# A windowed-attention and SwiGLU layer on one core: the softmax sink as a 129th key, a group's norm in four pieces, and another PSUM buffer for the transposed probabilities

## The chip, the cores and the metric

One core of a Trainium2 chip runs the whole layer. The metric is the time on the device, in microseconds (us), from the start to the end of one execution; the value of a kernel is the median of several runs. The engines are named as in the profile: PE is the matrix engine (PEld its weight loads), DVE the vector engine, ACT the scalar engine, POOL the GpSimd engine, SP the engine that only issues transfers. All data is float32; products on PE are made in split form, high part and low part.

## What is computed

The input x has 512 rows (tokens) of 2048. With one layer, only attention and the feed-forward part run:

```python
h = rms_norm(x, mixer_norm)
x = x + sliding_window_attention(h, ...)      # 32 query heads of 64, 4 key/value heads, window 128
x = x + swiglu(rms_norm(x, ffn_norm), ...)    # 2048 -> 5632 -> 2048
```

Inside attention, for each block of 128 queries, its own 128 keys and the 128 before them:

```python
scores = einsum('bnqhgd,bnkhd->bnhgqk', qb, kw) * scale      # masked to the window
m = maximum(max(scores), sink)                               # one sink number per head
p = exp(scores - m)
probs = p / (sum(p) + exp(sink - m))
out = einsum('bnhgqk,bnkhd->bnqhgd', probs, vw)
```

Queries and keys are normed per head (mean square over the 64 numbers) and rotated before the scores.

## The kernel before

The program is one list of events. `ev(t, fn)` puts a piece of code at time t, counted in weight tiles (256 rows by 512 columns of a weight matrix), and `run_events` calls the pieces in order of t. PE executes in that order. The order on DVE and ACT is not that of the calls: after the first four tiles a scheduler orders both engines when the program is built, by its own estimate of what is ready; `soon()` gives a piece a high priority in it. POOL and SP keep queues of their own. Each engine works its queue strictly in order.

The first 40 weight tiles make keys and values (tiles 0 to 7) and then queries, 8 tiles for each of the four key/value groups; tiles from 40 on are the output projection. One weight tile is 24 products of 128x512 (`tok_mm`, L144 in the profile), and ACT and DVE split each tile into `whi` and `wlo` ahead of it.

The attention of a group g is laid between the products of the next tiles, in class `Group`. E is the event time at which the group's queries are complete. `evac` copies them out of PSUM; `stat` squares them on ACT, sums the squares on DVE (`qss`) and makes the factor `f8` with `head_factor`, 13 short DVE operations each needing the one before; `q_prep` rotates a block's queries (POOL makes `rt`, DVE multiplies and adds into `qraw`) and splits them into `qs`; `k_exp` and `k_tr` do the same for the keys (`kx`, `kT`). A group has eight units, called u0 to u7 here: four blocks b, two halves hf of four heads. The units of the next group are marked with a prime, so u0' follows u7. The stretch in which u4 to u7 of one group, the norm of the next and its u0' and u1' come together is called a turn; there are three, in order turn 1, 2 and 3. A unit's chain is:

- `q_tr`: PE transposes four heads' queries into a PSUM tile, ACT copies them to `qT`;
- `soft`: PE makes the scores `sc`; ACT copies the last 128 keys' columns to `p`; DVE puts the earlier keys' columns over them where the mask says so (the predicated copy); DVE finds the maximum `mx`; ACT takes the exponentials with their sum `sm`; DVE divides;
- `p_tr`: PE transposes `p` into the PSUM tile `pT`; ACT copies the high part `ph`, DVE makes the low part `pl`; POOL selects `uh` and `ul` from them for the earlier block's keys;
- `pv`: PE multiplies with the values into the PSUM tile `po`, in four products (`ph`, `pl`, `uh`, `ul`); ACT (`oh`) and DVE (`attT`) bring it out.

PSUM has eight banks. Four hold the running products (`accA`), two the scores (`psc`, one buffer of two banks), and two are the buffers of `pst`, tag t1, in turn for `ptr` of queries, `ptr` of keys, `pT` and `po`. An engine that writes a new tile into a buffer waits until all readers of the old tile are done. The events of a unit stand at u - 0.78 (`q_tr`), u (`soft`), u + 1.43 (`p_tr`) and u + 1.99 (`pv`), with u 0.98 apart from unit to unit, so `p_tr` of one unit falls between the scores of the next two.

Of the kernel before, what the change touches and what calls it, by code (L numbers as in the profile page):

```python
# [19 lines left out]
P = 128  # L20
# [4 lines left out]
HD = 64  # L25
# [21 lines left out]
def hybrid_layer(ctx, tc, x, positions, inv_freq, mixer_norm, ffn_norm, w_qkv, q_norm, k_norm, sinks,  # L47
# [136 lines left out]
    nsink = cp.tile([P, 32], F32, name="nsink")  # L184
# [13 lines left out]
    warm = ap_.tile([P, 512], F32R, tag="qT", name="warm", bufs=3)  # L198
# [86 lines left out]
    tabs = {}  # L285

    def tables():
        dve.tensor_scalar(nsink, sink_b, -1.0, None, ALU.mult)
# [137 lines left out]
    class Group:  # L426
# [8 lines left out]
                copy_r(qr, qb[self.g + 1][t])  # L435
                self.qraw.append(qr)

        def stat(self):
            qss = ap_.tile([P, 32], F32, tag="qss", name="qss", bufs=2)
            for t in range(NT):  # L440
                sq = ap_.tile([P, 512], F32, tag="sq", name="sq")
                act.activation(sq, self.qraw[t], AF.Square)
                dve.tensor_reduce(qss[:, 8 * t:8 * t + 8], sq.rearrange("p (h d) -> p h d", d=HD), AX.X, ALU.add)
            fa = ap_.tile([P, 32], F32, tag="fa", name="fa")
            fb = ap_.tile([P, 32], F32, tag="fb", name="fb")
            self.f8 = ap_.tile([P, 32], F32, tag="f8", name="f8", bufs=2)
            head_factor(self.f8, qss, fa, fb, rs8, 8)

        def k_exp(self):
            g = self.g  # L450
            kx = ap_.tile([P, 2, NT, 2, HD], F32R, tag="qs", name="kx", bufs=2)
            s4 = kc[:, :, g * HD:(g + 1) * HD].unsqueeze(2).to_broadcast([P, NT, 2, HD])
            copy_r(kx[:, 0], s4)
            sub(kx[:, 1], s4, kx[:, 0].bitcast(F32))
            self.kx = kx
# [19 lines left out]
        def q_tr(self, b, hf):  # L475
            ptr = pst.tile([P, 512], F32R, tag="t1", name="ptr")
            for h in range(4):
                pe.transpose(ptr[:, h * P:(h + 1) * P],
                             self.qs[b][:, hf * 4 + h, :, :].rearrange("p c d -> p (c d)"), identr)
            qT = ap_.tile([P, 512], F32R, tag="qT", name="qT", bufs=3)  # L480
            with soon():
                copy_r(qT, ptr.bitcast(F32))
            self.qT[b, hf] = qT

        def soft(self, b, hf):

            h0 = self.g * GRP + hf * 4
            sc = psc.tile([P, 4, 256], F32, tag="sc", name="sc")
            lo_ = 0 if b else P
            qT = self.qT.pop((b, hf))  # L490
            for h in range(4):
                q_ = qT[:, h * P:(h + 1) * P]
                ks = slice((b - 1) * P + lo_, (b + 1) * P)
                mm(sc[:, h, lo_:256], q_, self.kT[0][:, ks], True, False)
                mm(sc[:, h, lo_:256], q_, self.kT[1][:, ks], False, True)
            p_ = ap_.tile([P, 4, P], F32, tag="p", name="p", bufs=3)
            mb = mask.unsqueeze(1).to_broadcast([P, 4, P])
            with soon():
                copy_r(p_, sc[:, :, P:256])
                if b:  # L500
                    dve.copy_predicated(p_, mb, sc[:, :, 0:P])
                else:
                    dve.copy_predicated(p_, mb, negc.unsqueeze(2).to_broadcast([P, 4, P]))
            mx = ap_.tile([P, 4], F32, tag="mx", name="mx", bufs=3)
            sm = ap_.tile([P, 4], F32, tag="sm", name="sm", bufs=3)
            es = ap_.tile([P, 4], F32, tag="es", name="es", bufs=3)
# [11 lines left out]
            dve.tensor_tensor(p_, p_, sm.unsqueeze(2).to_broadcast([P, 4, P]), ALU.mult)  # L518
            self.p[b, hf] = p_

        def p_tr(self, b, hf):
            p_ = self.p.pop((b, hf))
            pT = pst.tile([P, 512], F32, tag="t1", name="pT")
            for h in range(4):
                pe.transpose(pT[:, h * P:(h + 1) * P], p_[:, h, :], ident)  # L525
# [12 lines left out]
            self.pt[b, hf] = (ph, pl, pu)  # L538
# [19 lines left out]
                dve.tensor_tensor(attT[up, b, kt0:kt0 + 2, :], o4[up, :, 1, :], oh[up], ALU.add)  # L558

    LAG, PACE, TQ, QP = 2.6, 0.98, 0.78, 1.39  # L560
    TT, TP = 1.43, 1.99
    KX, KA, KB = 3.03, 1.98, 0.28
    for g in range(NKV):
        G = Group(g)
        E = 8 * (g + 2)
        ev(E - 0.0005, G.evac)
        ev(E + 0.01, G.stat)
        ev(E - KX, G.k_exp)
        ev(E - KA, lambda G=G: G.k_tr(0))
        ev(E - KB, lambda G=G: G.k_tr(1))  # L570
# [619 lines left out]
```

## Time and profile before

| | |
|---|---|
| median of 3 runs | 1877.29 us (1876.54 to 1877.72) |
| the profiled execution | 1877.08 us, span 1875.4 us |
| mean granted clock of PE | 0.997 |
| busy in the span | PE 1851.9 us, DVE 1500.3, ACT 878.2, POOL 146.8 |
| chain that ended last, by engine | PE 88%, DVE 7%, ACT 3% |

Busy time is the sum of an engine's instructions; matmuls are pipelined, so a busy PE can still lose a little at each stop. The chain that ended last is followed back from the last instruction, at each step to what released it. PE is busy in nearly all of the span; the attention units lie between 120 and 400 us.

### The profile page before, as it was taken

What the parts mean: (1) busy time and instruction counts of PE and PEld (TensorE: products, weight loads), DVE (VectorE), ACT (ScalarE), POOL (GpSimd) and SP (SyncE); (2) the same over time, 40 slices, a digit from 0 to 9 for tenths busy, and PEclk for the clock granted to TensorE, in tenths of its full rate; (3) what the DMA queues carried; (4) which work ended last, traced back from release to release, by engine and by line L of the source; (5) the groups of instructions that cost most, each with busy time, mean ns of one, the idle gap of its engine ahead of it and who ended that gap; (6) DMA issues with size and microseconds to landing.
All of it is one profiled execution on the core that took longest, in us unless ns stands there. A gap on an engine that the chain in (4) does not pass through costs nothing.

```text
span 1875.4 us, 32539 instructions
## 1 busy us (share of the span) xinstructions
PE 1851.9 (99%) x13118; PEld 1735.8 (93%) x13118; DVE 1500.3 (80%) x2422; ACT 878.2 (47%) x1347; POOL 146.8 (8%) x183
## 2 busy tenths in 40 slices
PE   8999999999999999999999999999999999999999
PEld 6887877788889999999999999999998999899899
DVE  4568898864686888888888888888889888988987
ACT  5458788754453333334333333433435434534532
POOL 0012122110000000000000000000000011012011
PEclk8999999999999999999999999999999999999999
DMA  6322211134413333333333333333345556646664
GB/s 205 90 79 59 67 56 59 66 128 170 168 57 96 124 119 119 124 115 122 113 113 123 125 114 120 118 113 116 125 131 186 163 133 151 198 127 137 175 183 135
DMA packets 162967, 230.81 MB, mean 123 GB/s; under 512 B 10141, under 2 KB 109537, under 8 KB 162305
## 3 DMA queue, kind: packets, MB, share of 16 engines
q1 hardware_dynamic: 146400, 194.81, 32.1%
q0 software_dynamic: 15552, 32.61, 7.6%
q8 instruction: 102, 1.67, 0.4%
q10 hardware_dynamic: 864, 1.33, 0.2%
q14 instruction: 49, 0.39, 0.1%
HBM read 200.39 MB, written 31.46 MB: 124 GB/s over the span
## 4 chain that ended last, share of the span: by engine, by line
PE 88%; DVE 7%; ACT 3%; issue 1%; DMA 1%; POOL 0%; ACTq 0%; DVEq 0%
PE acc L144 85%; PE sc L144 1%; DVE wlo L70 1%; PE po L144 1%; ACT p L513 1%; DVE hlo L70 0%; DVE dwl L70 0%; PE pT L525 0%; DVE sums L70 0%; PE pt L691 0%; DVE pl L70 0%; PE pt L250 0%; DVE mx L507 0%; DMA raw<-actd 0%; DVE sl L70 0%
## 5 line engine op out<-in xcount | busy, mean ns | idle before, releaser
L65 ACT ACTIVATE Whi<-W 128x1792 fp32r<-128x1792 f32 x168 | 286.5, 1705 | 518.3 <-PE acc L144 263.0
L70 DVE TENSOR_TENSOR Wlo<-W,Whi 128x1792 fp32r<-128x1792 f32 x168 | 340.4, 2026 | 133.2 <-ACT Whi L65 129.0
L144 PE MATMUL acc<-sh,Wlo 128*128 128x256 f32 x1344 | 380.3, 283 | 0.0
L144 PE MATMUL acc<-sh,Whi 128*128 128x256 f32 x1344 | 380.3, 283 | 0.0
L144 PE MATMUL acc<-sl,Whi 128*128 128x256 f32 x1344 | 380.3, 283 | 0.0
L144 PE MATMUL acc<-hhi,Wlo 128*128 128x256 f32 x1008 | 285.4, 283 | 0.5 <-DVE Wlo L70 0.5
L144 PE MATMUL acc<-hlo,Whi 128*128 128x256 f32 x1008 | 285.3, 283 | 0.0
L144 PE MATMUL acc<-hhi,Whi 128*128 128x256 f32 x1008 | 285.3, 283 | 0.0
L144 PEld LDWEIGHTS acc<-sh,Wlo 128*128 128x128 f32 x1344 | 258.0, 192 | 0.0
L144 PEld LDWEIGHTS acc<-sh,Whi 128*128 128x128 f32 x1344 | 258.0, 192 | 0.0
L144 PEld LDWEIGHTS acc<-sl,Whi 128*128 128x128 f32 x1344 | 258.0, 192 | 0.0
L144 PE MATMUL acc<-whi,hhi 128*128 128x512 f32 x512 | 209.0, 408 | 0.8 <-ACT hhi L67 0.8
L144 PE MATMUL acc<-whi,hlo 128*128 128x512 f32 x512 | 202.3, 395 | 0.0
L144 PE MATMUL acc<-wlo,hhi 128*128 128x512 f32 x512 | 201.5, 394 | 0.0
L144 PEld LDWEIGHTS acc<-hhi,Wlo 128*128 128x128 f32 x1008 | 193.5, 192 | 0.7 <-DVE Wlo L70 0.7
L144 PEld LDWEIGHTS acc<-hhi,Whi 128*128 128x128 f32 x1008 | 193.5, 192 | 0.0
L144 PEld LDWEIGHTS acc<-hlo,Whi 128*128 128x128 f32 x1008 | 193.5, 192 | 0.0
L70 DVE TENSOR_TENSOR W<-W 128x512 f32<-128x512 f32 x336 | 185.9, 553 | 7.6 <-DMA W<-ffn_w_up_in 1.1
L144 PE MATMUL acc<-dwh,sh 128*128 128x256 f32 (+1 forms) x600 | 180.1, 300 | 0.2 <-ACT row L65 0.2
L144 PE MATMUL acc<-dwl,sh 128*128 128x256 f32 (+1 forms) x600 | 180.0, 300 | 0.0
L144 PE MATMUL acc<-dwh,sl 128*128 128x256 f32 (+1 forms) x600 | 180.0, 300 | 0.0
L144 PE MATMUL acc<-dwh,hlo 128*128 128x256 f32 (+1 forms) x500 | 150.1, 300 | 0.0
(288 smaller groups left out, 3572.1 us busy)
## 6 DMA issues: line engine op xcount, KB each, us to landing
W<-ffn_w_up_in SPq DMA_DIRECT2D x176, 256.0 KB, 3.1
dw<-ffn_w_down_in SPq DMA_DIRECT2D x88, 512.0 KB, 3.6
W<-ffn_w_gate_in SPq DMA_DIRECT2D x160, 256.0 KB, 3.0
wraw<-attn_w_qkv_in SPq DMA_DIRECT2D x39, 512.0 KB, 3.6
wraw<-attn_w_o_in SPq DMA_DIRECT2D x32, 512.0 KB, 3.5
actd<-U POOLq DMA_DIRECT2D x22, 512.0 KB, 3.5
raw<-actd SPq DMA_DIRECT2D x22, 512.0 KB, 4.4
x1d<-row POOLq DMA_DIRECT2D x44, 256.0 KB, 5.7
```

The costliest lines, as they stand in the source:

```text
L65: act.activation(dst, src, AF.Copy)
L70: dve.tensor_tensor(dst, a, b, ALU.subtract)
L144: pe.matmul(ps, lhsT, rhs, start=start, stop=stop, skip_group_check=True)
L513: act.activation(p_[:, h, :], p_[:, h, :], AF.Exp, bias=mx[:, h:h + 1], scale=ff[:, h:h + 1], accum_out=sm[:, h:h + 1])
```

## The change

- **Sink.** The tile `p` gets a 129th column per head. POOL fills it with the sink divided by the unit's factor (`sf`), so that the maximum over 129 columns and the exponentials' sum over 129 columns already hold the sink. Three DVE operations on 128x4 numbers per unit (the minimum with `nsink`, `es`, and the addition to `sm`) and one exponential on ACT go; a POOL copy of 128x4 per unit comes. The maximum is multiplied by `nf`, the negated factor.
- **Norm.** `stat` runs once per token tile, at E + 0.01, 0.31, 0.61 and 0.91, and `factor` at E + 1.3 makes `f8`, `nf` and `sf`: three more DVE operations on 128x32 numbers per group.
- **PSUM.** `pT` is no longer a t1 tile; it takes the one scores buffer, so scores, `pT`, scores, `pT` follow each other in it.
- **Keys.** `kx` has a tile of its own in place of a `qs` buffer; `k_exp` moves from E - 3.03 to E - 3.9, the two `k_tr` from E - 1.98 and E - 0.28 to E - 2.83 and E - 1.85.
- `p` and `qT` go from three buffers to two; `pv` from u + 1.99 to u + 2.04.

```diff
-        def stat(self):
-            qss = ap_.tile([P, 32], F32, tag="qss", name="qss", bufs=2)
-            for t in range(NT):
-                sq = ap_.tile([P, 512], F32, tag="sq", name="sq")
-                act.activation(sq, self.qraw[t], AF.Square)
-                dve.tensor_reduce(qss[:, 8 * t:8 * t + 8], sq.rearrange("p (h d) -> p h d", d=HD), AX.X, ALU.add)
+        def stat(self, t):
+            if t == 0:
+                self.qss = ap_.tile([P, 32], F32, tag="qss", name="qss", bufs=2)
+            sq = ap_.tile([P, 512], F32, tag="sq", name="sq")
+            act.activation(sq, self.qraw[t], AF.Square)
+            dve.tensor_reduce(self.qss[:, 8 * t:8 * t + 8], sq.rearrange("p (h d) -> p h d", d=HD), AX.X, ALU.add)
+
+        def factor(self):
...
+            head_factor(self.f8, self.qss, fa, fb, rs8, 8)
+            dve.tensor_scalar(self.nf, self.f8, -1.0, None, ALU.mult)
+            dve.reciprocal(self.sf, self.f8)
+            sv = self.sf.rearrange("p (t h) -> p t h", h=GRP)
+            dve.tensor_tensor(sv, sv, sink_b[:, self.g * GRP:(self.g + 1) * GRP].unsqueeze(1)
+                              .to_broadcast([P, NT, GRP]), ALU.mult)
...
-            kx = ap_.tile([P, 2, NT, 2, HD], F32R, tag="qs", name="kx", bufs=2)
+            kx = ap_.tile([P, 2, NT, 2, HD], F32R, tag="kx", name="kx")
...
-            p_ = ap_.tile([P, 4, P], F32, tag="p", name="p", bufs=3)
+            p_ = ap_.tile([P, 4, P + 4], F32, tag="p", name="p", bufs=2)
+            pk, pa = p_[:, :, 0:P], p_[:, :, 0:P + 1]
+            pool.tensor_copy(p_[:, :, P:P + 1], self.sf[:, f_].unsqueeze(2))
...
-            dve.tensor_reduce(mx, p_, AX.X, ALU.max)
-            ff = self.f8[:, 8 * b + 4 * hf:8 * b + 4 * hf + 4]
-            dve.tensor_tensor(mx, mx, ff, ALU.mult)
-            dve.scalar_tensor_tensor(mx, mx, -1.0, nsink[:, h0:h0 + 4], ALU.mult, ALU.min)
-            dve.tensor_tensor(es, sink_b[:, h0:h0 + 4], mx, ALU.add)
+            dve.tensor_reduce(mx, pa, AX.X, ALU.max)
+            dve.tensor_tensor(mx, mx, self.nf[:, f_], ALU.mult)
             for h in range(4):
-                act.activation(p_[:, h, :], p_[:, h, :], AF.Exp, bias=mx[:, h:h + 1],
+                act.activation(pa[:, h, :], pa[:, h, :], AF.Exp, bias=mx[:, h:h + 1],
                                scale=ff[:, h:h + 1], accum_out=sm[:, h:h + 1])
-            act.activation(es, es, AF.Exp)
-            dve.tensor_tensor(sm, sm, es, ALU.add)
...
-            pT = pst.tile([P, 512], F32, tag="t1", name="pT")
+            pT = psc.tile([P, 4, 256], F32, tag="sc", name="pT")[:, 0:2, :].rearrange("p a b -> p (a b)")
...
-    TT, TP = 1.43, 1.99
-    KX, KA, KB = 3.03, 1.98, 0.28
+    TT, TP = 1.43, 2.04
+    KX, KA, KB = 3.9, 2.83, 1.85
...
-        ev(E + 0.01, G.stat)
+        for t in range(NT):
+            ev(E + 0.01 + 0.3 * t, lambda G=G, t=t: G.stat(t))
+        ev(E + 1.3, G.factor)
```

The scheduler answers to this with another order on DVE. In turn 2, before the low part `pl` of u4 (pl_2524 before), DVE has the first sum of squares and the rotation of the next group's first block:

```order
L507 TENSOR_REDUCE mx_2457<-p_2454 128x4
...
L511 TENSOR_TENSOR es_2459<-sink_b_82,mx_2457 128x4
L443 TENSOR_REDUCE qss_2554<-sq_2555 128x8
L341 TENSOR_TENSOR qraw_2531<-qraw_2531,t1q_465 128x512
L342 TENSOR_TENSOR qraw_2531<-qraw_2531,rt_2593 128x512
L70 TENSOR_TENSOR pl_2524<-pT_2518,ph_2523 128x512
L516 TENSOR_TENSOR sm_2458<-sm_2458,es_2459 128x4
```

With the change the same three operations stand behind it (pl_2476 is now the low part of u4, p_2417 is u5's probabilities, p_2539 u6's):

```order
L516 TENSOR_REDUCE mx_2421<-p_2417 128x4
...
L70 TENSOR_TENSOR pl_2476<-pT_2470,ph_2475 128x512
L521 RECIPROCAL sm_2422<-sm_2422 128x4
L522 TENSOR_TENSOR p_2417<-p_2417,sm_2422 128x4x128
L70 TENSOR_TENSOR wlo_2496<-wraw_2302,whi_2495 128x512 x2
L442 TENSOR_REDUCE qss_2506<-sq_2507 128x8
L339 TENSOR_TENSOR qraw_2483<-qraw_2483,t1q_463 128x512
L511 COPY_PREDICATED p_2539<-mask_86,sc_2530 128x4x128
L442 TENSOR_REDUCE qss_2506<-sq_2516 128x8
L340 TENSOR_TENSOR qraw_2483<-qraw_2483,rt_2522 128x512
```

One sum and two wide operations have moved from ahead of `pl` of u4 to behind it. Further on in turn 2, DVE comes to u0' (p_2768) and to the low part of u7 (pl_2804) with the change like this:

```order
L348 TENSOR_TENSOR f8_2620<-fa_2618,rs8_85 128x32
L513 COPY_PREDICATED p_2768<-mask_86,negc_87 128x4x128
L449 TENSOR_SCALAR nf_2621<-f8_2620 128x32
L450 RECIPROCAL sf_2622<-f8_2620 128x32
L339 TENSOR_TENSOR qraw_2489<-qraw_2489,t1q_463 128x512
L452 TENSOR_TENSOR sf_2622<-sf_2622,sink_b_82 128x32
L70 TENSOR_TENSOR hlo_143<-attT_153,hhi_142 128x4x128
L516 TENSOR_REDUCE mx_2772<-p_2768 128x4
L70 TENSOR_TENSOR wlo_2812<-wraw_2607,whi_2811 128x512
L70 TENSOR_TENSOR pl_2804<-pT_2798,ph_2803 128x512
```

The three new operations of the factor lie on both sides of the predicated copy, and the maximum behind them needs the sink column that POOL copies out of `sf`. Before, `f8` of this group was complete sixteen rows ahead of the same copy.

## Rows read from the trace of the kernel before

**Rows 1.** The page: busy time, share of the span and instructions of each engine.

```profile
PE 1851.9 (99%) x13118; PEld 1735.8 (93%) x13118; DVE 1500.3 (80%) x2422; ACT 878.2 (47%) x1347; POOL 146.8 (8%) x183
```

**Rows 2.** Who PE waited for, whole span: total us, times, longest us.

```profile
PE ptr L460 <- DVE attT L558: 3.1, 3, 1.0
PE pT L525 <- DVE attT L558: 2.9, 4, 0.9
...
PE po L144 <- POOL ul L535: 2.1, 6, 0.4
PE po L144 <- DVE pl L70: 1.9, 2, 1.1
...
PE pT L525 <- ACT qT L65: 1.5, 3, 0.5
```

**Rows 3.** Busy us by stretch: PE, PEld, DVE, ACT, POOL, clock, DMA.

```profile
126.00:134.00 8.00, 8.00 (x47) 6.89 (x46) 3.34 (x9) 5.89 (x15) 0.00 (x0) 1.00 0.23 66
246.00:254.00 8.00, 7.20 (x37) 5.54 (x36) 7.92 (x20) 7.04 (x20) 3.70 (x4) 1.00 0.16 57
...
270.00:278.00 8.00, 6.43 (x35) 4.83 (x34) 7.89 (x20) 6.31 (x21) 1.22 (x2) 1.00 0.20 66
```

**Rows 4.** PE in order of time, turn 2: start, us, tile, [idle before <-releaser].

```profile
237.40 0.51 PE L460 MATMUL ptr<-identr,kx 128*128 128x128 f32 x4 [1.03 <-DVE attT L558]
...
263.45 1.00 PE L144 MATMUL sc<-kT,qT 128*128 128x128 f32 x8
...
266.78 0.60 PE L525 MATMUL pT<-ident,p 128*128 128x128 f32 x4
...
271.52 0.50 PE L144 MATMUL po<-pl,v3l 128*128 128x512 f32 x1 [1.13 <-DVE pl L70]
...
280.94 1.12 PE L144 MATMUL sc<-kT,qT 128*128 128x256 f32 x8
```

**Rows 5.** DVE in order of time, turn 2; same columns.

```profile
240.53 0.69 DVE L70 TENSOR_TENSOR pl<-pT,ph 128x512 fp32r<-128x512 f32 x1 [0.45 <-ACT ph L65]
...
246.80 0.67 DVE L507 TENSOR_REDUCE mx<-p 128x4 f32<-128x512 f32 x1
247.39 0.68 DVE L341 TENSOR_TENSOR qraw<-qraw,t1q 128x512 f32<-128x512 f32 x1
...
249.36 0.15 DVE L510 SCALAR_TENSOR_TENSOR mx<-mx,nsink 128x4 f32<-128x4 f32 x1
249.44 0.68 DVE L70 TENSOR_TENSOR hlo<-attT,hhi 128x512 fp32r<-128x512 f32 x1
...
267.07 0.80 DVE L503 COPY_PREDICATED_SCALAR p<-mask,negc 128x512 f32 x1
...
272.05 0.59 DVE L511 TENSOR_TENSOR es<-sink_b,mx 128x4 f32<-128x4 f32 x1
...
280.28 0.69 DVE L70 TENSOR_TENSOR pl<-pT,ph 128x512 fp32r<-128x512 f32 x1
```

**Rows 6.** One of DVE's groups, 126 to 400 us: busy us, mean ns, idle before.

```profile
L516 DVE TENSOR_TENSOR sm<-sm,es 128x4 f32<-128x4 f32 x32 | 6.5, 203 | 15.6 <-ACT es L515 15.5
```

**Rows 7.** POOL in order of time: `ul` in a quiet stretch, in turn 2.

```profile
231.81 0.64 POOL L535 TENSOR_SCALAR_AFFINE_SELECT ul<-pl 128x512 fp32r<-128x512 f32 x1 [0.30 <-DVE pl L70]
...
271.53 1.10 POOL L535 TENSOR_SCALAR_AFFINE_SELECT ul<-pl 128x512 fp32r<-128x512 f32 x1 [1.41 <-DVE mx L510]
```

**Rows 8.** DVE in order of time, a quiet unit of group 0.

```profile
139.01 0.69 DVE L70 TENSOR_TENSOR pl<-pT,ph 128x512 fp32r<-128x512 f32 x1 [0.81 <-ACT ph L65]
...
141.69 0.73 DVE L501 COPY_PREDICATED p<-mask,sc 128x512 f32<-128x512 uint8 x1
```

**Rows 9.** PE in order of time, the same unit.

```profile
136.69 0.60 PE L525 MATMUL pT<-ident,p 128*128 128x128 f32 x4
...
139.90 1.12 PE L144 MATMUL sc<-kT,qT 128*128 128x256 f32 x8
...
144.47 0.60 PE L525 MATMUL pT<-ident,p 128*128 128x128 f32 x4
```

More of the change, by code (lines that the diff above doesn't have):

```diff
@@ L183, in hybrid_layer @@
     sink_b = cp.tile([P, 32], F32, name="sink_b")
-    nsink = cp.tile([P, 32], F32, name="nsink")
     rstd = cp.tile([P, NT], F32, name="rstd")
@@ L197, in hybrid_layer @@
     xt = xp.tile([P, NT, D], F32, tag="X", name="xt")
-    warm = ap_.tile([P, 512], F32R, tag="qT", name="warm", bufs=3)
+    warm = ap_.tile([P, 512], F32R, tag="qT", name="warm", bufs=2)
     pool.memset(warm.bitcast(F32), 0.0)
@@ L287, in tables @@
     def tables():
-        dve.tensor_scalar(nsink, sink_b, -1.0, None, ALU.mult)
         dve.tensor_copy(pos_f, pos_i)
@@ L436, in evac @@
                 self.qraw.append(qr)
-        def stat(self):
-            qss = ap_.tile([P, 32], F32, tag="qss", name="qss", bufs=2)
-            for t in range(NT):
-                sq = ap_.tile([P, 512], F32, tag="sq", name="sq")
-                act.activation(sq, self.qraw[t], AF.Square)
-                dve.tensor_reduce(qss[:, 8 * t:8 * t + 8], sq.rearrange("p (h d) -> p h d", d=HD), AX.X, ALU.add)
+        def stat(self, t):
[5 more added lines that the diff above has]
+        def factor(self):
             fa = ap_.tile([P, 32], F32, tag="fa", name="fa")
             fb = ap_.tile([P, 32], F32, tag="fb", name="fb")
-            self.f8 = ap_.tile([P, 32], F32, tag="f8", name="f8", bufs=2)
-            head_factor(self.f8, qss, fa, fb, rs8, 8)
+            self.f8, self.nf, self.sf = [ap_.tile([P, 32], F32, tag=n, name=n, bufs=2) for n in ("f8", "nf", "sf")]
+            head_factor(self.f8, self.qss, fa, fb, rs8, 8)
[4 more added lines that the diff above has]
+                              .to_broadcast([P, NT, GRP]), ALU.mult)
         def k_exp(self):
             g = self.g
-            kx = ap_.tile([P, 2, NT, 2, HD], F32R, tag="qs", name="kx", bufs=2)
+            kx = ap_.tile([P, 2, NT, 2, HD], F32R, tag="kx", name="kx")
             s4 = kc[:, :, g * HD:(g + 1) * HD].unsqueeze(2).to_broadcast([P, NT, 2, HD])
@@ L479, in q_tr @@
                              self.qs[b][:, hf * 4 + h, :, :].rearrange("p c d -> p (c d)"), identr)
-            qT = ap_.tile([P, 512], F32R, tag="qT", name="qT", bufs=3)
+            qT = ap_.tile([P, 512], F32R, tag="qT", name="qT", bufs=2)
             with soon():
@@ L485, in soft @@
         def soft(self, b, hf):
-            h0 = self.g * GRP + hf * 4
             sc = psc.tile([P, 4, 256], F32, tag="sc", name="sc")
@@ L495, in soft @@
                 mm(sc[:, h, lo_:256], q_, self.kT[1][:, ks], False, True)
-            p_ = ap_.tile([P, 4, P], F32, tag="p", name="p", bufs=3)
+            p_ = ap_.tile([P, 4, P + 4], F32, tag="p", name="p", bufs=2)
+            pk, pa = p_[:, :, 0:P], p_[:, :, 0:P + 1]
+            f_ = slice(8 * b + 4 * hf, 8 * b + 4 * hf + 4)
+            ff = self.f8[:, f_]
+            pool.tensor_copy(p_[:, :, P:P + 1], self.sf[:, f_].unsqueeze(2))
             mb = mask.unsqueeze(1).to_broadcast([P, 4, P])
             with soon():
-                copy_r(p_, sc[:, :, P:256])
+                copy_r(pk, sc[:, :, P:256])
                 if b:
-                    dve.copy_predicated(p_, mb, sc[:, :, 0:P])
+                    dve.copy_predicated(pk, mb, sc[:, :, 0:P])
                 else:
-                    dve.copy_predicated(p_, mb, negc.unsqueeze(2).to_broadcast([P, 4, P]))
+                    dve.copy_predicated(pk, mb, negc.unsqueeze(2).to_broadcast([P, 4, P]))
             mx = ap_.tile([P, 4], F32, tag="mx", name="mx", bufs=3)
             sm = ap_.tile([P, 4], F32, tag="sm", name="sm", bufs=3)
-            es = ap_.tile([P, 4], F32, tag="es", name="es", bufs=3)
-            dve.tensor_reduce(mx, p_, AX.X, ALU.max)
-            ff = self.f8[:, 8 * b + 4 * hf:8 * b + 4 * hf + 4]
-            dve.tensor_tensor(mx, mx, ff, ALU.mult)
-            dve.scalar_tensor_tensor(mx, mx, -1.0, nsink[:, h0:h0 + 4], ALU.mult, ALU.min)
-            dve.tensor_tensor(es, sink_b[:, h0:h0 + 4], mx, ALU.add)
+            dve.tensor_reduce(mx, pa, AX.X, ALU.max)
+            dve.tensor_tensor(mx, mx, self.nf[:, f_], ALU.mult)
             for h in range(4):
-                act.activation(p_[:, h, :], p_[:, h, :], AF.Exp, bias=mx[:, h:h + 1],
+                act.activation(pa[:, h, :], pa[:, h, :], AF.Exp, bias=mx[:, h:h + 1],
                                scale=ff[:, h:h + 1], accum_out=sm[:, h:h + 1])
-            act.activation(es, es, AF.Exp)
-            dve.tensor_tensor(sm, sm, es, ALU.add)
             dve.reciprocal(sm, sm)
-            dve.tensor_tensor(p_, p_, sm.unsqueeze(2).to_broadcast([P, 4, P]), ALU.mult)
+            dve.tensor_tensor(pk, pk, sm.unsqueeze(2).to_broadcast([P, 4, P]), ALU.mult)
             self.p[b, hf] = p_
@@ L522, in p_tr @@
             p_ = self.p.pop((b, hf))
-            pT = pst.tile([P, 512], F32, tag="t1", name="pT")
+            pT = psc.tile([P, 4, 256], F32, tag="sc", name="pT")[:, 0:2, :].rearrange("p a b -> p (a b)")
             for h in range(4):
-                pe.transpose(pT[:, h * P:(h + 1) * P], p_[:, h, :], ident)
+                pe.transpose(pT[:, h * P:(h + 1) * P], p_[:, h, 0:P], ident)
             ph = ap_.tile([P, 512], F32R, tag="ph", name="ph", bufs=2)
```

## The prediction

> **What bounds the kernel now.** I read the page first, then the list of what PE waited for, then the busy times by stretch, and last the instructions in order of time where PE stood. PE is busy 1851.9 of 1875.4 us [rows 1], and the change leaves every product and transposition in place. What the change can give or take is therefore time in which PE stands. In the attention part PE stands for a t1 buffer that `po` has not left (3.1 and 2.9 us) or that `qT` has not (1.5), and for `pl` and `ul` ahead of the value products (1.9 and 2.1): 11.5 us in all [rows 2]. That is the most that removing waits can bring.
>
> The stretches tell where. In a quiet one PE is busy 8.00 of 8 us with DVE at 3.34 (a unit without an earlier block; later ones lie higher). In turn 2, from 246 to 254 and from 270 to 278, DVE is at 7.92 and 7.89 of 8, and PE falls to 7.20 and 6.43 [rows 3]. So a turn is a place where DVE has no time left, and PE waits for what DVE has not come to. In order of time turn 2 begins with a wait of PE that is not DVE's load: `ptr` of the keys stands 1.03 us at 237.40, because the t1 buffer before it is still `po`. DVE then makes `pl` of u4 at 240.53, having stood 0.45 us for ACT, and from there it works nearly without a stop to `pl` of u0' at 280.28 [rows 4, 5]. A shorter list of DVE work between these two is worth time; a longer one costs it.
>
> **The change part by part.** *The keys' transposition.* `k_tr(1)` moves 1.57 tiles earlier and `pT` no longer takes t1 buffers, so nothing close ahead of it holds its buffer. Its wait of 1.03 us goes in each turn, and `pl` of u4 comes that much sooner: -1.03. The operations themselves cost PE the same elsewhere; `kx` is computed before the turn both times.
>
> *The sink.* Between `pl` of u4 and `pl` of u0' each turn holds four units, so twelve 128x4 operations go. Their price has two ends. Where DVE does not have to wait for its own last result, the next operation starts 0.08 us later (249.36 to 249.44, [rows 5]); the mean of one over all units is 0.20 [rows 6]. I take 0.12, nearer the first, because in a turn other work stands between them: 12 x 0.12 = 1.44 us less. In quiet stretches DVE has idle time anyway, and the exponential that leaves ACT is covered as well: nothing there.
>
> *The norm.* Three new 128x32 operations of `factor` come, at the same 0.12: 0.36 us more. Spread `stat` changes the order: one sum and the two rotation operations of the first block, which DVE did before `pl` of u4, stand behind it now (the first two order lists). Such operations start 0.59 us after each other (246.80 to 247.39, [rows 5]); 3 x 0.60 = 1.8 us more in the full stretch. Their old place was in time that DVE partly has to spare, so moving them is no gain there.
>
> Sum for DVE between the two low parts: 1.8 + 0.36 - 1.44 = +0.72 us per turn; with the small ones at 0.08 it is +1.08, at 0.20 it is 0. The counts of rows are the same in all three turns.
>
> *The transposed probabilities in the scores' buffer.* New waits: `pT` waits until the scores before it have been copied, the next scores until `pl` has read `pT`. Of u0' in turn 2 the predicated copy ends at 267.07 + 0.80 = 267.87, but `pT` of u7 started at 266.78 [rows 4, 5]. That `pT` must now wait about 1.1 us. Behind it PE reaches `pl` of u7 later by as much, so its 1.13 us there [rows 4] mostly vanish: one wait takes the place of the other, and q_tr, the next products and `sc` of u1' wait behind it. At the turn's end the scores of u2' started at 280.94, when `pl` of u0' was just ending (280.28 + 0.69 = 280.97). Today that is no condition; afterwards it is. So the turn ends when DVE's list ends: -1.03 + 0.72 = -0.31 us per turn, -0.9 for three.
>
> In quiet units the same waits are met: `pl` ends at 139.70 [rows 8] and the next scores start at 139.90 [rows 9], the predicated copy ends at 141.69 + 0.73 = 142.42 [rows 8] and the next `pT` starts at 144.47 [rows 9]. No cost, with 0.20 us to spare at the narrowest. After turn 3 the last small wait for `attT` in rows 2 goes: -0.2.
>
> *The POOL copies.* Thirty-two of 128x4. No POOL operation that small is in the trace. Lower end: nothing, as POOL has idle time and the copy is issued long before the maximum, except for u0', where it follows `sf`. Upper end: `ul` took 0.64 us in a quiet stretch and 1.10 in the turn [rows 7], and a 128x4 operation of DVE beside that one took 0.59 (272.05) instead of 0.15 (249.36) and held its successor some 0.5 us [rows 5]. So a POOL operation that reads SBUF can cost DVE up to 0.5 us. I take 0, as the copy moves 4 numbers per partition where the select moves 512; 12 of them in the three turns at 0.5 are the upper bound, 6.
>
> The page "SBUF — State Buffer" of the Trainium skill, section "SBUF: two separate sides", speaks against the change here: DVE with two SBUF inputs and a reading GpSimd operation share one pair of ports, which the first takes for its whole instruction. By that rule a copy holds DVE only for its own length or is held itself; rows 7 agree on the blocking, and no row shows the copy's length.
>
> *Buffers.* `p` and `qT` with two buffers: `p_tr` of a unit stands 0.53 tile ahead of the scores two units on, and `soft` 1.18 tiles ahead of the `q_tr` two units on. Both are free by PE's own order. If that cover were gone each would cost an ACT copy's length per unit.
>
> Sum: -0.9 - 0.2 = -1.1 us against the profiled execution's own 1877.08 us, so 1876.0; that execution lies 0.2 below the median of 1877.29, so **1876.2** for the median.
>
> **The rivals.** *A: the waits go (faster).* If DVE is not as full as I read it, because the longer list is taken up by the time that the earlier `pT` and `po` give, the 11.5 us of [rows 2] vanish and only the new wait of 1.1 us at u7 is left in each turn: 11.5 - 3.3 = 8.2 us, 1868.9 (1869.1 for the median). For it: DVE has time to spare outside the turns, and t1 loses a third of its users. Against it: 7.92 and 7.89 of 8 [rows 3]. The decisive point is whether DVE idles between the two low parts.
>
> *B: the POOL copies hold DVE (slower).* Place: the turns, where DVE has no reserve. Price: 0.5 us each by [rows 5, 7], four per turn, 6.0 us in all, so 1876.2 + 6.0 = 1882.2. It decides the sign from 0.1 us per copy, and makes the kernel measurably slower from 0.4 us. For it: the maximum of u0' waits for a copy that itself waits for `sf`. Against it: the size.
>
> *C: the one scores buffer binds every unit.* If `pl` or the copy comes 0.5 us later than in the quiet unit of [rows 8, 9], 0.3 us are lost in each of some 24 quiet units, 7.2 us: 1883.4. Against it: DVE's list in quiet units only gets shorter.
>
> *D: the change does not do what it says.* The rows that move are in the built order; nothing speaks for it.
>
> **How the numbers follow.** Forecast 0.47, A 0.30, B 0.17, C 0.06, D 0. About 0.2%, 3.75 us, is what a measurement of this kernel can tell from no change. The forecast's own range goes with the small operations' price, from 0.20 (0 in place of +0.72: -1.03 x 3 = -3.1, less the 0.2 of the end: 1874.0) to 0.08 (+0.05 x 3: 1877.2). For 8 in 10 I reach to A and to B: **1869 to 1882**. Faster: A and a small part of the forecast, 0.35; slower: most of B and C, 0.19; within 0.2%: 0.46.
>
> **What would show it.** Right: PE's waits for `ptr` of the keys are gone; new waits of about 1 us appear at `pT` of u7 and at scores, ended by the predicated copy or by `pl`; DVE stays above 7.8 of 8 us in the turns; PE's standing time in 120 to 400 us is within 2 us of before. For A, PE's standing time there is below 5 us and DVE idles in the turns. For B, wide DVE operations of 1.1 us or more stand beside the copies. I am wrong altogether if PE's time outside the attention part moves.

## The result and the profile after

The changed kernel takes 1862.59 us (median of 6 runs, 1857.58 to 1870.94) beside 1877.49 for the kernel before (6 runs, 1876.54 to 1879.25): a ratio of 0.9926, 95% interval 0.991 to 0.9943, so it is faster by 0.7%, 14.9 us. The forecast was 1876.2; its range ended at 1869. The profiled execution of the changed kernel is one of its longer ones, 1869.77 us with a span of 1868.0. Where the text below says "ratio", it is to the kernel before, run on the same chip in the same session. Three executions of other runs that stand far out of line (above 1970 us, one each in e13, e15 and e17) are left out of every list, median and ratio.

The page of the changed kernel, busy time by engine, against [rows 1]:

```profile
PE 1846.9 (99%) x13118; PEld 1729.6 (93%) x13118; DVE 1489.4 (80%) x2337; ACT 874.5 (47%) x1315; POOL 153.4 (8%) x215
```

PE issues the same 13118 products and is busy 5.0 us less. So most of what this execution gained is no wait that went; the products themselves take less time. Who PE waited for in the changed kernel (total us, times, longest), against [rows 2]:

```profile
PE po L144 <- DVE pl L70: 6.6, 3, 2.5
...
PE sc L144 <- DVE pl L70: 1.7, 2, 1.1
```

The waits of `ptr` and `pT` (3.1, 2.9 and 1.5 us before) are gone, and nearly as much stands in one place instead: `po` for `pl` 6.6 in place of 1.9, and the scores for `pl` 1.7. Busy time by stretch (PE, PEld, DVE, ACT, POOL, granted clock, DMA), against [rows 3]:

```profile
246.00:254.00 8.00, 7.43 (x39) 5.97 (x38) 7.88 (x15) 7.90 (x23) 5.86 (x7) 1.00 0.07 25
270.00:278.00 8.00, 7.57 (x42) 6.20 (x41) 7.95 (x18) 6.12 (x20) 0.86 (x2) 1.00 0.19 66
```

DVE is as full in the turn as before. From the first scores to the last, the attention part takes 266.5 us in the place of 266.7. The gain lies later. The same columns for 800 us of the SwiGLU part, in the kernel before and in the changed one:

```profile
600.00:1400.00 800.00, 800.00 (x6669) 800.00 (x6668) 669.08 (x897) 308.27 (x218) 11.21 (x21) 1.00 0.37 119
```

```profile
600.00:1400.00 800.00, 800.00 (x6722) 800.00 (x6722) 674.34 (x903) 309.70 (x219) 11.20 (x21) 1.00 0.38 121
```

PE never stands in either and the clock is full, but 53 products more fit in. The part works in rounds of 21 products (seven sub-products of three): 800 x 21 / 6669 is 2519 ns a round, 800 x 21 / 6722 is 2499. Read from the starts of the rounds' first products, all but the first rounds take 2520 ns in the one and 2500 in the other, each to the nanosecond or so. From the first of the 336 rounds to the last there are 335 such steps, so 335 x 0.020 = 6.7 us of this execution's 7.3. The page "Perfetto Trace Analysis" of the Trainium skill, section "Identifying the Most-Contended Engine", says that the share of time in which products are busy is no good measure of how near PE is to its limit; these rows agree, at 800.00 of 800 us in both.

Nothing in the SwiGLU part was edited. What differs there is where tiles lie. In a partition of SBUF the constants lie at the low end, and after them `hhi`, `hlo`, the rows, the weights and later `W`, `Whi`, `Wlo`, `dwh` and `dwl`; the attention pool, later `ohi` and `olo`, and then `sh` and `sl` are laid from the high end. The change removes the constant `nsink`, 128 bytes per partition. In the built programs `hhi` goes from 18400 to 18272 and `Whi` from 108512 to 108384, while `ohi` stays at 155616 and `sh` at 163808. Before, these four leave the rest 224 when divided by 256 (modulo 256); afterwards the two low ones leave 96. Below, two tiles lie alike where this rest is the same, and apart where it is not. The tiles inside the attention pool moved too, by the new sizes of `p`, `qT` and `kx`.

### The profile page after: what moved, and what is told of

Its sections match the earlier page's. It is cut to its first block, busy times and chain, and to the rows that moved or that the text cites. A ratio compares the mean times of both kernels' runs of the same rounds, so it can differ in the third digit from the quotient of the medians.

```text
span 1868.0 us, 32559 instructions
## 1 busy us (share of the span) xinstructions
PE 1846.9 (99%) x13118; PEld 1729.6 (93%) x13118; DVE 1489.4 (80%) x2337; ACT 874.5 (47%) x1315; POOL 153.4 (8%) x215
## 4 chain that ended last, share of the span: by engine, by line
PE 91%; DVE 5%; ACT 2%; issue 1%; POOL 0%; DMA 0%; ACTq 0%; DVEq 0%; POOLq 0%
PE acc L144 88%; DVE wlo L70 1%; PE sc L144 1%; PE po L144 1%; DVE qraw L339 0%; PE pT L530 0%; DVE pl L70 0%; PE pt L249 0%; DVE qss L442 0%; ACT p L519 0%; PE pt L698 0%; DVE qraw L340 0%; PE ptr L484 0%; DMA small<-ffn_norm_in 0%; DVE qs L70 0%
## 5 line engine op out<-in xcount | busy, mean ns | idle before, releaser
L144 PEld LDWEIGHTS acc<-sh,Wlo 128*128 128x128 f32 x1344 | 252.7, 188 | 0.0
L144 PEld LDWEIGHTS acc<-hhi,Wlo 128*128 128x128 f32 x1008 | 189.7, 188 | 0.8 <-DVE Wlo L70 0.8
L144 PEld LDWEIGHTS acc<-hhi,Whi 128*128 128x128 f32 x1008 | 189.7, 188 | 0.0
L144 PEld LDWEIGHTS acc<-hlo,Whi 128*128 128x128 f32 x1008 | 189.0, 187 | 0.0
```

Of the source, the lines that this page charges most:

```text
L144: pe.matmul(ps, lhsT, rhs, start=start, stop=stop, skip_group_check=True)
```

## Experiments: where the tiles lie

Theory **place**: the gain outside the attention part comes from this shift. Rival **order**: it comes from the changed instructions of the attention part, by the state in which that part hands over. A third theory, **restart**, came with the results: where tiles lie apart modulo 256, several steady patterns of a round are possible, and the last wait of PE picks one. In the diffs, a tile named `pad`, `fpad` or `opad` takes its place in SBUF and is never read or written.

**e1_before_nsink_moved.** The kernel before, with the new line as the first tile of the attention pool:

```diff
-    nsink = cp.tile([P, 32], F32, name="nsink")
+    nsink = ap_.tile([P, 32], F32, name="nsink")
```

> The kernel before, with the tile nsink (128 bytes per partition) taken from the constants and put at the low end of the attention pool: no instruction is added, removed or moved, but hhi, hlo, the weights' tiles, W, Whi, Wlo, dwh and dwl lie 128 bytes lower, as they do in the changed kernel, while ohi, olo, sh and sl stay. Theory 'place' (the gain comes from where the tiles lie): 1857 to 1871 us, and in the SwiGLU part the products of 256 columns start less than 120 ns after each other (119.05 on average in the changed kernel), those of 512 columns with sh some 232 ns in place of 227. Rival 'order' (the gain comes from the attention part's instructions, by the state in which it hands over to the later part): 1877.4 us within 1, and every 256-column product at 120 ns.

**e2_after_pad128**, and **e3_after_pad64** with 16 in place of 32. The changed kernel:

```diff
     sink_b = cp.tile([P, 32], F32, name="sink_b")
+    pad = cp.tile([P, 32], F32, name="pad")
```

> The changed kernel with an unused tile of 128 bytes per partition among the constants, so that the tiles of the later parts lie where they lie in the kernel before. Place: the SwiGLU products are back at 120 ns each, and what is left is the change of the attention part alone, 1876.2 us as forecast from its steps, 1875 to 1877. Order: 1862.6 us as the changed kernel, 1857 to 1871, pitch 119.05 ns.

> The changed kernel with 64 unused bytes per partition among the constants: left-hand tiles lie half way between their places in the two kernels. Place: another time than both is possible; if the distance counts in steps of 128 bytes the pitch is one of the two, 119.05 or 120 ns, if finer, a third value. Order: 1862.6, 1857 to 1871.

**e4_after_sink_moved.** The changed kernel, the new line again at the low end of the attention pool:

```diff
-    sink_b = cp.tile([P, 32], F32, name="sink_b")
+    sink_b = ap_.tile([P, 32], F32, name="sink_b")
```

> The changed kernel with sink_b moved from the constants to the low end of the attention pool: left-hand tiles lie 128 bytes lower again, 256 below the kernel before. Place, if only the distance modulo 256 bytes counts: 120 ns and 1876 as after_pad128; if larger distances count: a time of its own, below 1876. Order: 1862.6, 1857 to 1871.

The four ran in one session. Low tiles are given by their distance from their place in the kernel before.

| run | low tiles | us | ratio, 95% interval | products in 600 to 1400 us |
|---|---|---|---|---|
| e1 | -128 | 1871.95 | 0.9964 (0.9953 to 0.9976) | 6723 |
| e2 | 0 | 1876.68 | 0.9995 (0.9985 to 1.0004) | 6669 |
| e3 | -64 | 1872.33 | 0.9969 (0.9959 to 0.9979) | 6686 |
| e4 | -256 | 1877.77 | 1.0001 (0.9991 to 1.001) | 6669 |

The windows of e1 and of e2:

```profile
600.00:1400.00 800.00, 800.00 (x6723) 800.00 (x6722) 674.47 (x903) 309.84 (x219) 11.20 (x21) 1.00 0.38 121
```

```profile
600.00:1400.00 800.00, 800.00 (x6669) 800.00 (x6668) 669.46 (x897) 308.28 (x218) 11.20 (x21) 1.00 0.38 119
```

That decides it. The kernel before gets the shorter round without any change of an instruction, and the changed kernel loses it when 128 bytes that nobody uses are put back. Half the shift gives a third value (2513 ns), twice the shift is as none: of these distances, 256 bytes count as 0. Order is out as the cause of the shorter round. And e2 is what the prediction was about: the change with the tiles of all later parts in their places takes 1876.68 us. Of the expectations, the median of e1 lay 1 us above its range.

Next, which tiles have to lie apart. **e5_after_again** is the changed kernel as it is. **e6_whi_apart** is e2, and **e7_hhi_apart** the changed kernel, each with

```diff
     s_dma(2)
+    fp.tile([P, 32], F32, name="fpad")
     gs = []
```

and **e8_ohi_alike** is the changed kernel with a pad below the pool of `ohi` and `olo`, closed with it:

```diff
+        olw.enter_context(tc.tile_pool(name="opad", bufs=1, side="right")).tile([P, 32], F32, name="opad")
         last_o[0] = olw.enter_context(tc.tile_pool(name="wo_last", bufs=1, side="right", reuse_waits="tile"))
```

> The changed kernel itself, unchanged, beside the other three. Place alone, with the attention part's 1.6 us between the medians of the run with 128 unused bytes and the kernel before: 1872 (the run with nsink moved) less 0.9 to 1.6, so 1870 to 1871, pitch 119.05 ns in the SwiGLU part as in its first profile. Rival: place and the changed attention part together give more than both apart, 1857 to 1866.

> The run with 128 unused bytes among the constants, with 128 unused bytes more between W and Whi: Whi and Wlo now lie 128 bytes (modulo 256) from both hhi, hlo and sh, sl; all else lies as in the kernel before. If a product of 256 columns is shorter where its moving rows and its weights lie apart modulo 256: all 21 of a round shorten, 2500 ns or less a round against 2520, so 6.7 us or more less than 1876.7: 1870 or less, and the 512-column products stay at 227. If what shortens them is that the products with hhi and those with sh differ from each other: 120 ns and 1876.7.

> The changed kernel with 128 unused bytes between W and Whi: hhi and hlo lie apart (128 modulo 256) from Whi, Wlo, sh and sl, which lie alike. If a product is shorter where its moving rows and its weights lie apart: the nine of 21 with hhi or hlo shorten, those with sh stay at 120. If the change from one to the other counts (moving rows of the product that runs, weights of the next): as the changed kernel, near 119.05. The 512-column products with sh in the down part stay at 232, as in the changed kernel.

> The changed kernel with 128 unused bytes above the last output weights, so that ohi and olo lie 128 bytes lower, alike with hhi modulo 256 as in the kernel before. Place: the 192 products of ohi and olo with 512 columns take 227 ns again in place of 233, 1.1 us less in all than the changed kernel run beside it. Rival (the longer products come from something else, as a DMA at that time): 233 as in the changed kernel.

| run | what lies apart (128 modulo 256) | us (range) | ratio, 95% interval | products |
|---|---|---|---|---|
| e5 | hhi, Whi from sh | 1869.76 (1868.98 to 1871.78) | 0.9952 (0.9938 to 0.9967) | 6723 |
| e6 | Whi from hhi and sh | 1866.44 (1864.70 to 1868.43) | 0.9933 (0.9919 to 0.9948) | 6744 |
| e7 | hhi from Whi and sh | 1869.44 (1867.56 to 1870.89) | 0.9946 (0.9929 to 0.9962) | 6740 |
| e8 | as e5; ohi alike with hhi | 1865.14 (1860.62 to 1871.16) | 0.9928 (0.9901 to 0.9956) | 6795 |

All three ways of lying apart beat lying alike; e5 lay 0.2 us below its expected range. e6 came out as the first theory in its expectation says (2492 ns). e7 contradicts the finer picture: products with `sh`, which were to stay at 120 ns, start 118 to 119 ns after each other like those with `hhi`; what one product gains, its neighbours show, and no cost belongs to one product alone.

For 512 columns lying apart costs time. The output projection's `ohi` products of the changed kernel and of e8 (min/median/max ns):

```profile
L144 PE MATMUL acc<-ohi,hhi x64: 390/394/477, 474.1 to 523.4; 128*128 128x512 f32 x64
```

```profile
L144 PE MATMUL acc<-ohi,hhi x64: 389/389/478, 475.0 to 523.1; 128*128 128x512 f32 x64
```

From start to start it is 233 ns against 227, over some 192 products 1.1 us, and moving that one pool takes it back, as expected. In the down part, the last of SwiGLU, the 288 products of 512 columns with `sh` and `sl` go from 227 to 232 ns as well, and some 1500 of 256 columns there get shorter, some 1.5 us each way, so that the part gains nothing clear. But e8 did something that nobody expected: its traced execution has rounds of 2473 ns, though no tile of the SwiGLU part moved, and its four times are two near 1861 and two near 1870. So place is not all.

## Experiments: which pattern an execution gets

The traces hold a hint. In the third round PE stands for `Wlo`; this is e6:

```profile
576.20 0.39 PE L144 MATMUL acc<-hhi,Wlo 128*128 128x256 f32 x1 [0.52 <-DVE Wlo L70]
```

The rounds ahead of this wait take 2527 and 2520 ns in e6, all behind it 2492 on average; in e8, 2500 ahead and 2473 behind. **e12_no_restart** (the changed kernel) and **e13_whi_no_wait** (e6) take the wait away by splitting those weights earlier:

```diff
-            s_split(i + 1)
+            if i:
+                s_split(i + 1)
...
     s_sums(1)
     s_split(0)
+    s_dma(3)
+    s_split(1)
```

> The changed kernel with the second split of up weights put ahead of the gate's activation, so that PE no longer stands 0.8 us for Wlo in the second round of 21 products. Theory 'restart' (tiles that lie apart allow several steady patterns, and the one that follows this wait lasts to the part's end): the pattern of the first rounds, 2500 ns, stays, all runs 1868 to 1871 less 0.8, none near 1861. Rival (the pattern is drawn elsewhere or may change at any place): runs at 1860 to 1862 beside such at 1868 to 1871, as in the run with ohi alike.

> The run with Whi and Wlo apart, with PE's wait for Wlo in the second round of the SwiGLU part taken away as in the run without that wait. There the first two rounds took 2527 and 2520 ns, and those after the wait 2492. Restart (the wait picks the pattern): the rounds stay at 2520 ns, so 332 times 28 ns, 9.3 us, come back and 0.8 us go: 1866.4 + 8.5 = 1875. Rival (places alone give the pattern): 2492 ns soon after the start, 1865.6.

e12: 1868.38 us (1865.34 to 1869.68), ratio 0.9941 (0.9926 to 0.9956), every round 2500 ns in its traced execution. e13: 1877.20 us (nine executions, 1872.78 to 1881.18), ratio 0.9992 (0.9983 to 1.0002), where e6 with the same places had 0.9933. The windows of e6 and of e13:

```profile
600.00:1400.00 800.00, 800.00 (x6744) 800.00 (x6743) 675.19 (x903) 311.23 (x220) 11.19 (x21) 1.00 0.38 121
```

```profile
600.00:1400.00 800.00, 800.00 (x6670) 800.00 (x6668) 669.32 (x894) 306.48 (x217) 10.66 (x20) 1.00 0.37 118
```

Taking away a wait of 0.5 us cost 9 to 11: the rounds stayed in the pattern of the first ones, 2520 ns, to the end of the part. So in e6 places alone do not give the shorter round; with the wait it comes behind it and stays, and in the run without the wait it never comes. That it is the wait itself which counts, as restart says, is the likely reading, but the edit also moves one split to an earlier place on ACT and DVE, and no run separates the two. e12 fits it and shows less: its first rounds had 2500 ns anyway, and only the lack of an execution near 1861 among its four speaks.

Three runs look at how often each comes. **e15_after_five** and **e18_after_look** are the changed kernel unchanged, **e16_ohi_five** is e8.

> The changed kernel once more, in five rounds. If the pattern varies from execution to execution on one chip: times near 1870 and near 1861 in one list. If it belongs to a chip or a session: all of one kind, as the four runs of 1869 to 1872 before.

> The run with ohi and olo alike, in five rounds, beside the changed kernel. If the pattern varies from execution to execution: times near 1869 and near 1860 in one list, as in its first four. If the changed kernel beside it shows one kind only, the later start of the SwiGLU part (1.1 us earlier here) takes part in picking the pattern.

> The changed kernel again, for its trace. If its executions near 1861 are those with rounds of 2473 ns: a traced execution below 1865 has 2473, one above 1868 has 2500. Rival (another cause in the attention or the down part): a traced execution below 1865 with rounds of 2500 ns.

e15: 1860.75, 1862.34, 1863.85, 1864.12 and 1869.58. e16: 1857.71, 1860.51, 1860.54, 1861.11, 1867.79 and 1868.69, ratio 0.9915 (0.9897 to 0.9932). By their times both kinds come from one program on one chip, and the first six runs of the changed kernel divide the same way (1869.77 and 1870.94; four from 1857.58 to 1863.23). Of its 17 executions in all, ten lie from 1857.58 to 1864.12 us and seven from 1868.98 to 1871.78. e18 was traced at 1860.97 us:

```profile
600.00:1400.00 800.00, 800.00 (x6795) 800.00 (x6794) 680.29 (x910) 314.84 (x224) 11.19 (x21) 1.00 0.38 122
```

800 x 21 / 6795 is 2472 ns. So this shorter execution of the changed kernel has the pattern of 2473: its 332 rounds behind the wait take 47 ns less than in the kernel before, 15.5 us. The two longer ones that were traced (1869.77 and 1869.92) have 2500, 6.7 us, and e16, traced at 1860.51, has 2473 as e8. For the other executions the pattern is inferred from the time, and near 1865 the time does not tell: e12 was traced at 1865.34 with 2500. Why one restart ends in 2473 and another in 2500 is open: in both kinds DVE ends the wait, the rounds ahead take 2500 ns, the wait takes 0.57 us in traces with 2500 (the result's profile, e5) and 0.56 or 0.57 in those with 2473 (e8, e16, e18), and the rows around it show nothing that tells the kinds apart. No run was made that varies the length of this wait. The kernel before showed no such choice: with all tiles of this part alike, each traced program has 2520.

## Experiments: the parts of the change

**e9_sink_only** is the kernel before with the sink as the 129th key alone (the lines of the diff in `factor` and `soft`, `p` with three buffers, `nsink` as a pad). **e10_norm_whole** and **e11_pT_back** are e2 with one part undone each:

```diff
-        for t in range(NT):
-            ev(E + 0.01 + 0.3 * t, lambda G=G, t=t: G.stat(t))
-        ev(E + 1.3, G.factor)
+        ev(E + 0.01, lambda G=G: ([G.stat(t) for t in range(NT)], G.factor()))
```

```diff
-            pT = psc.tile([P, 4, 256], F32, tag="sc", name="pT")[:, 0:2, :].rearrange("p a b -> p (a b)")
+            pT = pst.tile([P, 512], F32, tag="t1", name="pT")
```

> The kernel before with the sink as the 129th key alone (the three operations per group that prepare it, the POOL copy, four operations per unit less); nsink stays as an unused tile, so the later parts' tiles do not move. By the prediction's step DVE's list between pl of u4 and pl of u0' gets shorter by 1.44 - 0.36 = 1.1 us in each turn; by the rows of the run with 128 unused bytes, in whose second turn the operations that went had held 3.3 us (es 1.18, sm+es 0.83, nsink 0.41, mx by f 0.85) and those that came 1.3 us (sf 0.78 and 0.10, nf 0.13, mx by nf 0.29), by 2.0. If DVE's list sets the turn's end, 1874 to 1871; if PE's waits only move to another place, 1876.5 to 1878. Rival B of the prediction (the POOL copies hold DVE): 1880 or more.

> The run with 128 unused bytes, with a group's norm in one piece again where the kernel before has it. By the prediction's step the spread put 1.8 us behind pl of u4 in each turn: 1.8 us less for DVE between pl of u4 and pl of u0' where it is full (the second turn), and 0 to 4 us less in all, 1873 to 1876.7. Rival: in one piece the norm stands ahead of pl of u4 and of the unit after it and holds them: PE waits there, and the time is 1877 to 1880.

> The run with 128 unused bytes, with pT in the t1 buffers again. By the prediction the scores' bank gives nothing by itself: pT's waits for attT and qT (2.9 and 1.5 us before) come back, the scores' waits for pl (1.6 us) go, and as DVE ends the turns the time stays within 1.5 us of 1876.7. Rival: the t1 waits put PE behind DVE's list in every turn: 1879 or more.

The turns are from `pl` of u4 to `pl` of u0' on DVE, in us:

| run | us | ratio, 95% interval | turns 1, 2, 3 |
|---|---|---|---|
| before | | | 37.29, 39.75, 39.49 |
| e2 | 1876.68 | 0.9995 (0.9985 to 1.0004) | 38.22, 39.05, 39.06 |
| e5 (tiles apart) | 1869.76 | 0.9952 (0.9938 to 0.9967) | 37.27, 39.06, 39.06 |
| e9 | 1878.84 | 1.0002 (0.9993 to 1.0012) | 36.89, 39.40, 40.54 |
| e10 | 1878.83 | 0.9999 (0.9989 to 1.0009) | 38.76, 39.84, 39.10 |
| e11 | 1875.50 | 0.9983 (0.9973 to 0.9992) | 37.29, 39.04, 39.30 |

A turn is read from one execution, and it varies: with the attention part of e2 unchanged, turn 2 took 39.05 or 39.06 us also in e3, e5, e8 and e18, but 39.49 in e6, 39.48 in e7 and 40.10 in e4.

e9: the sink alone gives no time. Its waits for `pl` grow from 1.9 to 5.3 us while those of `pT` shrink: they moved, as its second case says, though the time lies 0.8 us above the range given there. e10: the norm in one piece does not make turn 2 shorter by 1.8 us; the 0.79 by which it is longer is hardly more than the variation, and over the whole run the difference cannot be measured. e11: with `pT` back in t1 the kernel is faster than the one before by 0.17%, which e2 is not; so the scores' bank is the one part that looks like a cost: 0.0012 between the ratios of e2 and e11 are 2.3 us, with some 2.4 of uncertainty as they are of two sessions. Its waits are

```profile
PE po L144 <- DVE pl L70: 5.6, 3, 2.0
...
PE pT L531 <- ACT qT L65: 1.4, 3, 0.5
PE pT L531 <- DVE attT L564: 1.2, 2, 0.6
```

Last, the versions that the runs point to. **e14_whi_pT** is e6 with the edit of e11, **e17_ohi_pT** is e8 with it.

> The run with Whi and Wlo apart, with pT in the t1 buffers again as in the run with pT back. If the two gains add up: 1866.4 less 1.2 to 3.2 us (the run with pT back against the run with 128 unused bytes, 1875.5 and 1876.7, and by their ratios to the kernel before 0.9983 and 0.9995): 1863 to 1865, below the changed kernel beside it. If the start of the SwiGLU part picks another pattern there: rounds other than 2492 ns, and any time from 1858 to 1876.

> The run with ohi and olo alike, with pT in the t1 buffers again. If gains add up and the pattern falls as before: executions near 1859 and near 1867, the median with the larger group; 1.2 to 3.2 us below the run with ohi alike (1860.8 in five rounds): 1858 to 1860. If the start of the SwiGLU part picks the 2500 ns pattern more often: a median of 1866 to 1868.

e14: 1865.86 us, ratio 0.9931 (0.9919 to 0.9944), no better than e6, so the gain of e11 did not add up measurably there. e17: 1855.07, 1859.46 and 1864.56 us, ratio 0.9885 (0.9865 to 0.9904). It beats the kernel before. That it beats the changed kernel is not shown: in the same session that one, as e18, had 0.9908 (0.9888 to 0.9928), which overlaps, and three executions with two patterns among them are few. The trace of e17, of 1864.56 us, has the 2500 ns pattern.

## Why the prediction was wrong, point by point

**The step that failed** is the first paragraph's: "the change leaves every product and transposition in place. What the change can give or take is therefore time in which PE stands." The instructions stayed; the addresses did not. In the SwiGLU part, where PE never stands, a round of 21 products went from 2520 ns to 2500 or 2473. Removing `nsink` had no term in the sum and no rival, and it is worth 6.7 or 15.5 us in the SwiGLU part, by the pattern, less the 1.1 us that it costs the `ohi` products. The text's own mark was met: PE's time outside the attention part moved.

**The attention part** came out near its forecast: -1.1 us forecast, and e2, where the tiles of the later parts lie as before, has 0.9995 of the time before, -0.9 (-2.8 to +0.8), which cannot be told from nothing. That the sums agree is luck in part, for neither of the two terms of a turn (-1.03 and +0.72) was met:

*The keys' wait* went, as said: no `ptr` stands in the rows after. But `pl` of u4 did not come 1.03 us sooner by it. From `pl` of u0' in one turn to `pl` of u4 in the next, e2 takes 32.44 us ahead of turn 2, in place of 31.97 in the kernel before, and 31.39 ahead of turn 3, in place of 32.01. In turn 2 this `pl` waits for ACT's `ph` instead, 1.88 us, where it waited 0.45 before.

*DVE ends the turns.* Right for turn 2. There the list of e2 runs from the first to the last of these rows, and e3, e5 and e18 have the same 39.05 us within 0.02, whatever PE stood for in between:

```profile
241.24 0.69 DVE L70 TENSOR_TENSOR pl<-pT,ph 128x512 fp32r<-128x512 f32 x1 [1.88 <-ACT ph L65]
...
265.24 0.80 DVE L514 COPY_PREDICATED_SCALAR p<-mask,negc 128x512 f32 x1
...
280.30 0.69 DVE L70 TENSOR_TENSOR pl<-pT,ph 128x512 fp32r<-128x512 f32 x1
```

*Its length* was forecast at +0.72 us and came out at -0.70 in turn 2. The twelve operations that went had held, start to next start, 2.42 us in turn 2 of the kernel before (0.20 each, the upper of the two ends), not 1.44; and `mx` by the factor, which stayed, went from 0.85 to 0.29. The three of `factor` took 1.01, not 0.36; the moved sum and rotations 1.89, for which 1.8 stood. These come to -0.08 only. The 13 operations of `head_factor`, which both kernels have, took 1.45 us less, the wide `hlo` and `qs` 1.13 more, and all others 0.30 less: -0.70.

What the sum lacked is that a small operation has two lengths. Of the 34 small ones (128x4 and 128x32, the maxima aside) of this turn in the kernel before, 26 last 0.15 to 0.19 us and eight 0.53 to 0.73. Each of the eight runs beside an operation of POOL and ends within 0.06 us of the end of one, as `es` and `ul` do in [rows 5, 7] (272.64 and 272.63) and these two (253.46 and 253.42):

```profile
252.85 0.61 DVE L75 TENSOR_SCALAR fa<-fb 128x32 int32<-128x32 int32 x1
252.24 1.18 POOL L535 TENSOR_SCALAR_AFFINE_SELECT ul<-pl 128x512 fp32r<-128x512 f32 x1 [0.24 <-DVE pl L70]
```

In e2 one of 25 is that long; in e6 two are, and the second makes its 39.49 of 39.05. So in these traces the price of the small operations hangs on how many of them are caught beside POOL's, and that is what the sum's one price of 0.12 us missed. No run changes the POOL operations to test this.

*The new wait at `pT` of u7* did not come. PE in e2:

```profile
264.85 0.60 PE L531 MATMUL pT<-ident,p 128*128 128x128 f32 x4
268.05 0.40 PE L144 MATMUL po<-ph,v3h 128*128 128x512 f32 x1
270.38 0.51 PE L144 MATMUL po<-pl,v3l 128*128 128x512 f32 x1 [1.93 <-DVE pl L70]
```

`pT` starts before the predicated copy at 265.24. Of a unit without an earlier block that copy reads `mask` and `negc`, as its row says, and no scores; only ACT's copy has to leave the bank. The rows of before had said so [rows 5]: `p<-mask,negc`. The trade happened with the other partner: PE is no longer held ahead of `pl` of u7 and so stands 1.93 us there, for 1.13 before.

*The turn's end* is set by `pl` of u0' (the scores' wait of 1.1 us), as forecast.

*The clock* had no term. From the first scores to the last, e2 takes 266.6 us and e5 264.7, with the same instructions; 1.65 of these 1.9 us lie in turn 1 and the stretch up to turn 2, where the granted clock falls in e2 and not in e5 (rows at the end). That is more than the whole forecast.

**The rivals.** A: the waits did not go, 9.1 us of them stand in e2 in other places; DVE did not idle in turn 2. B: no. The copies in e2, one in a free stretch and one beside DVE:

```profile
240.15 0.19 POOL L507 COPY p<-sf 128x4 f32<-128x4 f32 x1 [2.70 <-PE pT L531]
...
248.91 0.66 POOL L507 COPY p<-sf 128x4 f32<-128x4 f32 x1
```

It takes 0.19 us by itself and 0.66 beside DVE's `qs` (248.83), which lasts 0.69 there as elsewhere, so it is the copy that is held; of the two ways that the prediction drew from the Trainium skill ("SBUF — State Buffer", section "SBUF: two separate sides") this is the harmless one. With the copies in, turn 2 got shorter. C: outside the turns the scores of one unit start 0.25 us late for it in e2; no more. D: no.

## What to carry to other kernels

Before costing a change at what it does to instructions, compare where the tiles lie: a constant of 128 bytes that goes moves every tile behind it, and where PE never stands, the start-to-start time of its products is the whole price. When a gain appears in a part that was not edited, test it first with the smallest edits, a pad in the changed kernel and the same shift in the old one; two runs separate place from order. And time such a kernel several times: one program can have more than one steady pattern. Price a small operation by what runs beside it in the stretch in question, not by its mean over the whole trace.

## What the runs showed of the hardware

- Start to start, a 256-column product took 120 ns on average with all tiles alike modulo 256 bytes, 119.05, 118.7 and 117.8 in patterns with tiles apart; a 512-column one 227 ns alike and 233 apart.
- A pattern, once reached, lasted 830 us, within 1 ns a round in e5 and 7 in e6. It changed at a wait of 0.5 us of PE in e6, from 2520 to 2492 ns, and stayed at 2520 in e13, where that wait was taken away.
- The same wait does not always bring the same clock. In turn 1 PE stands 2.5 us for `pl` in e2 and in e5 alike. Behind it the granted clock is at its lower level, 1.2 GHz, for a part of the window in e2 and never in e5 (the value after the engines' columns is the mean, 1.00 for 2.4 GHz):

```profile
200.00:206.00 6.00, 5.90 (x24) 4.75 (x24) 4.36 (x11) 3.39 (x12) 0.63 (x1) 0.72 0.30 87
```

```profile
200.00:206.00 6.00, 5.54 (x29) 4.43 (x30) 4.77 (x12) 4.34 (x15) 0.63 (x1) 1.00 0.30 87
```

  Turn 1 takes 38.22 us in the one and 37.27 in the other. In turn 2 the fall came in e5 and not in e2, and both took 39.06 within 0.01: there, where DVE ends the turn, the slow PE cost nothing. It does not always stay so. In turn 3 of e7 the clock is low for longer, and the turn takes 41.35 us, where e2, with a shorter fall, and e5, with none, have 39.06:

```profile
340.00:352.00 12.00, 10.82 (x36) 8.60 (x37) 8.77 (x17) 7.59 (x24) 0.97 (x1) 0.57 0.14 44
```
